# Two transformer blocks on one core: the gated branch's values and norm issued ahead of the convolution branch

## The chip, the cores and the metric

The kernel runs on one core of a Trainium2 chip. The metric is the device time of one execution in microseconds. Every time below is of this kernel on this chip. Engines are named as in the profile: PE does the matrix products (PEld its weight loads), DVE the tensor-tensor arithmetic, ACT the activations and copies, POOL little here, and SP issues the DMAs that bring weights in.

## What is computed

The program runs a first block on 512 tokens of width 1024, and then two layers of a second block, all in float32. The change lies in the first block's mixer, which is in the reference, cut to what matters:

```python
h = rms_norm(x, norm_mix_g[l]) * (1.0 + sc1) + sh1
p = h @ w_in[l]
y_a, v_first = rwkv7_mixer(p[..., :OFF_B], ...)
y_b = spatial_gating_mixer(p[..., OFF_B:OFF_C], ...)
y_c = short_conv_mixer(p[..., OFF_C:OFF_D], ...)
y_d = s5_mixer(p[..., OFF_D:OFF_G], ...)
merged = (gates[:, :, 0] * y_a + gates[:, :, 1] * y_b
          + gates[:, :, 2] * y_c + gates[:, :, 3] * y_d)
...
def spatial_gating_mixer(p, ln_w, ln_b, w_s, b_s, w_out):
    z = jax.nn.gelu(p)
    u = z[..., :D_MIX]
    v = layer_norm(z[..., D_MIX:], ln_w, ln_b, LN_EPS)
    v = v.reshape(bsz, seq // CHUNK, CHUNK, G_B, GROUP_B)
    mixed = jnp.einsum('gts,bnsgc->bntgc', w_s * mask, v) + b_s.T[None, None, :, :, None]
    return (u * mixed.reshape(bsz, seq, D_MIX)) @ w_out
def short_conv_mixer(p, conv_w, w_out):
    bg = p[..., :D_MIX]
    cg = p[..., D_MIX:2 * D_MIX]
    xin = p[..., 2 * D_MIX:]
    zp = jnp.pad(cg * xin, ((0, 0), (CONV_K - 1, 0), (0, 0)))
    y = sum(conv_w[j] * zp[:, j:j + seq] for j in range(CONV_K))
    return (bg * y) @ w_out
```

The four branches are independent of one another; all read `h`. The gated branch (`y_b`) has values `v` that are normalised and mixed over time, and gates `u`.

## The kernel before

Each float32 product is made of three products of rounded parts (`mm3`, L183): hi by hi, lo by hi, hi by lo. A weight tile is brought in by SP (`wload`, L159), ACT rounds it (whi, L160) and DVE takes the rest (wlo, L161); raw tiles have four buffers, whi and wlo three. `proj` is one such weight tile and 24 matmuls of 512 columns into one of three PSUM banks, which all products of the tag `mm` take in turn. `gelu2` (L251 to L261) is two ACT passes, two DVE passes, an ACT tanh and a DVE pass.

A scheduler puts the program's instructions into one fixed order for each engine; code written earlier has the better claim to an earlier place, and `issue_after` adds a bound to it. An engine then follows its own list and waits where something is missing.

`_first_block` (L1252) takes the mixer in this order:

- `_rwkv`: seven projections; during the sixth and seventh `_start_shift` (L476) makes the second version of `h`, eight tiles, each by DVE (L486, x), ACT (L488, hi) and DVE (L489, lo).
- `_s5_setup`: a long list of small DVE instructions on 128x8 tiles, held behind the last lo (L489).
- `_conv_branch` (L944): six projections, with a product of two (L950), two shifted taps (L957) and a gate (L959).
- `_sg_branch` (L965): first the small tables, then the values. Two weight tiles `w_in_v` (called kc 0 and 1) give 96 matmuls of 256 columns into four tiles `svp` (L979 to L984); four gelus, two norms (L996 to L1004), and the mark `sg_normed` (L1006). Then two tiles: a projection with gelu (`sgu`), the mixing (`sgm`, L1015), the bias (`sgx`, L1018), the gate (L1020) and a split.
- `_merge(K, 2, ...)`: eight output tiles, each a projection `gp` and six matmuls `yp`. Beside it, from the 27th piece on and held behind `sg_normed`, `_s5_tables` makes the tables Q and W by two `_cmul` (L1029 to L1034), twelve DVE instructions of 128x1024 elements, and then products `s5q` (L1118) and `s5k` (L1124).
- `_rwkv_shift`, `_s5_branch`, `_wkv` with the other merges, then the feed-forward part and the second block.

Of the kernel before, what the change touches and what calls it, by code (L numbers as in the profile page):

```python
# [100 lines left out]
class _Core:  # L101
# [15 lines left out]
    @contextmanager  # L117
    def tags(self, space=None, side=None, **n):

        before = dict(self.tag)  # L120
        kw = {} if space is None else {"space": space}
        if side is not None:
            kw["side"] = side
        self.npool += 1
        with self.tc.tile_pool(name=f"p{self.npool}", bufs=1, reuse_waits="tile", **kw) as p:
            self.tag.update({t: (p, c) for t, c in n.items()})
            try:
                yield
            finally:
                self.tag = before  # L130
# [209 lines left out]
def _ada(K, cols, tag=None, after=None):  # L340

    for j in cols:
        if tag is None:
            raw = K.wpool.tile([128, K.WMAX], F32, name="raw", tag="raw", bufs=4)[:, 0:1024]
        else:
            raw = K.g("ada_w", tag, shape=(128, 1024))
        _dot(K, raw, K.dram["ada_w"][j], K.c_row, K.modv[:, j:j + 1], 0.5, after)
        if j % 4 == 3:
            m = K.modv[:, j - 3:j + 1]
            K.nc.vector.tensor_tensor(m, m, K.vec("ada_b", j - 3, 4), OP.add)  # L350
        yield
# [592 lines left out]
def _conv_branch(K):  # L944
    nc, d = K.nc, K.dram
    z = []
    for i in range(2):
        cg = K.g("cg", "xr")
        nc.scalar.copy(cg, K.proj(d["w_in"][11 + 2 + i], K.h))
        nc.vector.tensor_tensor(cg, K.proj(d["w_in"][11 + 4 + i], K.h), cg, OP.mult)  # L950
        z.append(cg)
    out = []
    for i in range(2):
        y = K.g("cy", "xr")
        nc.scalar.activation(y, z[i], AF.Identity, scale=K.vec("conv_w", 4 + i))
        for j, sh in ((1, 1), (0, 2)):
            nc.vector.scalar_tensor_tensor(y[:, sh:], z[i][:, 0:S - sh], K.vec("conv_w", 2 * j + i), y[:, sh:],  # L957
                                           OP.mult, OP.add)
        nc.vector.tensor_tensor(y, K.proj(d["w_in"][11 + i], K.h), y, OP.mult)  # L959
        K.tap(f"yc{i}", y)  # L960
        out.append(K.split(y, "y"))
    return out


def _sg_branch(K, after):  # L965
    nc, d = K.nc, K.dram
    with K.tc.tile_pool(name="sgp", bufs=1, side="right") as sp:
        lnw = sp.tile([128, 2, 256], F32, name="sg_ln")
        bs = sp.tile([128, 2, 128], F32, name="sg_bs")
        ws = K._ld("sg_wsT", [128, 512], nc.sync, sp)  # L970
        for x in range(2):
            nc.sync.dma_start(lnw[:, x], d["sg_ln"][x].partition_broadcast(128))
        for g in range(4):
            nc.sync.dma_start(bs[(g % 2) * 64:(g % 2 + 1) * 64, g // 2], d["sg_bs"][g].partition_broadcast(64))
        w3 = ws.rearrange("p (g t) -> p g t", g=4)
        with K.tc.issue_after(after):
            nc.vector.tensor_tensor(w3, w3, K.tri.unsqueeze(1).to_broadcast([128, 4, 128]), OP.mult)
        vp = [K.mm("svp") for _ in range(4)]
        for kc in range(2):  # L979
            wh, wl = K.wload(d["w_in_v"][kc], 4, 256)  # L980
            for b in range(4):
                K.mm3(vp[b][:, 0:256],
                      [tuple(x[:, b * 128:(b + 1) * 128] for x in K.h[4 * kc + k]) for k in range(4)],
                      [(wh[:, k], wl[:, k]) for k in range(4)], first=kc == 0, last=kc == 1)  # L984
        vn = []
        for q in range(2):
            z = K.g("sgz", "xr")
            z3 = z.rearrange("p (b c) -> p b c", b=2)
            for b in range(2):
                K.gelu2(z3[:, b], vp[2 * q + b][:, 0:256], "xr", 256)  # L990
            st = K.col("bn_s", [128, 2, 6])
            ag = K.col("bn_a", [128, 2, 2])
            t, y = K.col("bn_t", [128, 2]), K.col("bn_y", [128, 2])
            ve = K.col("bn_v", [128, 2])
            for b in range(2):
                nc.vector.bn_stats(st[:, b], z3[:, b])  # L996
                nc.vector.bn_aggr(ag[:, b], st[:, b])
            nc.vector.tensor_scalar(ve, ag[:, :, 1], 0.25, 1e-5, OP.mult, OP.add)
            K.rsqrt(y, ve, t)
            nc.vector.tensor_scalar(y, y, 0.5, None, OP.mult)  # L1000
            for b in range(2):
                nc.vector.tensor_scalar(z3[:, b], z3[:, b], ag[:, b, 0:1], y[:, b:b + 1], OP.subtract, OP.mult)
                nc.vector.tensor_tensor(z3[:, b], z3[:, b], lnw[:, 0], OP.mult)
                nc.vector.tensor_tensor(z3[:, b], z3[:, b], lnw[:, 1], OP.add)  # L1004
                vn.append(z3[:, b])
        K.sg_normed = nc.cur_bb.bb.instructions[-1]  # L1006
        out = []
        for i in range(2):
            u = K.g("sgu", "xr")
            K.gelu2(u, K.proj(d["w_in"][7 + i], K.h), "xr")  # L1010
            ps = K.mm("sgm")
            for b in range(4):
                for h in range(2):
                    g = 2 * i + h
                    nc.tensor.matmul(ps[h * 64:(h + 1) * 64, b * 128:(b + 1) * 128],  # L1015
                                     lhsT=vn[b][:, g * 64:(g + 1) * 64], rhs=w3[:, g], start=True, stop=True)
            mx = K.g("sgx", "xr")
            nc.vector.tensor_tensor(mx.rearrange("p (b t) -> p b t", b=4), ps.rearrange("p (b t) -> p b t", b=4),  # L1018
                                    bs[:, i:i + 1].to_broadcast([128, 4, 128]), OP.add)
            nc.vector.tensor_tensor(mx, mx, u, OP.mult)  # L1020
            K.tap(f"yb{i}", mx)
            out.append(K.split(mx, "y", 0.5))
    return out


def _cmul(V, ore, oim, are, aim, bre, bim, t, conj=False):
# [225 lines left out]
def _first_block(K):  # L1252
    nc, d = K.nc, K.dram
    with ExitStack() as mix:
        tags = lambda **n: mix.enter_context(K.tags(**n))
        tags(h=16, y=8, yd=4, rk=8, cr=1)
        tags(space=PSUM, mm=3, sm=5)
        tags(side="right", tm=2)
        ada = _ada(K, range(16, 48))
        with K.tags(e=9, e4=8):  # L1260
            with K.tc.tile_pool(name="s5", bufs=1) as sp:
                tiles, rs = _rwkv(K, *_start(K))
                last = K.last
                with K.tc.issue_after(last), K.tc.issue_after(K.loaded):
                    z = _s5_setup(K, sp)
                yc = _conv_branch(K)
                yb = _sg_branch(K, last)
                acc = [K.g(f"acc{m}", "xr") for m in range(8)]
                for n, _ in enumerate(_merge(K, 2, yc, acc)):
                    if n == 26:  # L1270
                        with K.tc.issue_after(K.sg_normed):
                            tab = _s5_tables(K, sp, z)
                la, pairs = _rwkv_shift(K, tiles, rs)
            yd = _s5_branch(K, tab)
        with K.tags(rw=16, rw4=4), K.tc.tile_pool(name="rwc", bufs=1) as cp:
            la = _wkv_consts(K, cp, la)
            ya, mg = [], []
            fill = chain(_merge(K, 1, yb, acc), _merge(K, 3, yd, acc))
            for _ in range(PIECES_FIRST):
                next(fill, None)  # L1280
            for i in range(2):
                for n, _ in enumerate(_wkv(K, i, la, pairs[i][1], pairs[i][0], pairs[i][2], ya)):
                    for _ in range(int((n + 1) * PIECES) - int(n * PIECES)):
                        next(fill, None)
                    if n >= ADA_FROM and n % 2 == 0:
                        next(ada, None)
        for _ in fill:
            pass
        for _ in ada:
            pass  # L1290
        tags(mg=16)
        for _ in _merge(K, 0, ya, acc, mg):
            pass
        for m in range(8):
            K.tap(f"acc{m}", acc[m])
        K.xr = _load(K, "x", 8, "xr")
        for m in range(8):
            ps = K.proj(d["w_o"][m], mg)
            nc.vector.scalar_tensor_tensor(K.xr[m], ps, K.modv[:, 16 + m:17 + m], K.xr[m], OP.mult, OP.add)
            K.tap(f"xa{m}", K.xr[m])  # L1300
# [477 lines left out]
```

## Time and profile before

| | |
|---|---|
| median of 3 runs | 2137.5 us (2136.26 to 2139.16) |
| profiled execution | 2141.65 us |
| its span | 2139.9 us |
| mean granted clock of TensorE | 0.992 |
| PE busy | 2091.8 us, 98% |
| DVE busy | 1413.6 us, 66% |
| ACT busy | 934.5 us, 44% |
| DMA | 30.0% of 16 engines' span on the weight queue |

The span is what the profiler saw between the first and last instruction; 1.75 us of the profiled execution lie around it. Matmuls are pipelined, so each shows longer than its step: neighbours start 0.23 us apart where each is 0.39 us long. A group's "idle before" is time of that engine with nothing to do, and the arrow names what ended it. [...]

### The profile page before, as it was taken

Reading aid. Unit: us, or ns where it says so; the run is one execution under the profiler, and the core shown is the slowest. Engines: PE = TensorE matmul, PEld = TensorE weight load, DVE = VectorE, ACT = ScalarE, POOL = GpSimd, SP = SyncE. Lnnn points to the kernel's source line nnn. Section 1 sums busy time; section 2 is a strip of 40 time slices with the busy share of each in tenths; the row PEclk is TensorE's granted clock in tenths of the full one; section 3 lists DMA queues with packets and bytes.
Section 4 is the critical chain, followed back from the end, with each engine's and each line's share of the span. In section 5 each row is a group of like instructions: output and inputs, shape, how many; then the busy total and the mean of one; then the engine's idle time right before and its main releaser. Section 6 shows DMA issues by size and latency. Waiting matters only on the chain.

```text
span 2139.9 us, 29586 instructions
## 1 busy us (share of the span) xinstructions
PE 2091.8 (98%) x11542; PEld 1697.3 (79%) x11542; DVE 1413.6 (66%) x2651; ACT 934.5 (44%) x1551; POOL 21.9 (1%) x41
## 2 busy tenths in 40 slices
PE   7999999999999999999999999999999999999998
PEld 6878777778888888897778888888887678888887
DVE  7885886945644344567876756747668867575775
ACT  4433533324423232446774433424469954243433
POOL 0001000000000000000000000000000000000000
PEclk9989999999999999999999999999999999999999
DMA  8324353524322222242212322222421122323222
GB/s 319 113 72 142 107 164 104 178 88 137 111 99 93 95 99 91 97 122 87 80 60 89 99 97 91 99 93 80 136 79 41 60 79 86 102 84 105 97 81 67
DMA packets 68779, 220.47 MB, mean 103 GB/s; under 512 B 8500, under 2 KB 11604, under 8 KB 68640
## 3 DMA queue, kind: packets, MB, share of 16 engines
q1 hardware_dynamic: 65424, 210.72, 30.0%
q0 software_dynamic: 1920, 5.77, 0.9%
q8 instruction: 91, 1.49, 0.3%
q10 hardware_dynamic: 1296, 2.10, 0.3%
q14 instruction: 48, 0.39, 0.1%
HBM read 215.26 MB, written 3.30 MB: 102 GB/s over the span
## 4 chain that ended last, share of the span: by engine, by line
PE 86%; DVE 6%; ACT 4%; DMA 2%; issue 1%; SPq 0%; DVEq 0%; ACTq 0%
PE mm L183 63%; PE gp L183 7%; PE vt L183 3%; PE yp L183 2%; PE pT L1427 1%; PE po L1440 1%; DMA w_t<-w_in_t 1%; PE s L1407 1%; PE fin L183 1%; DVE wlo L161 1%; PE s L1408 1%; ACT p L1415 1%; ACT whi L160 1%; PE svp L183 1%; DVE raw L337 1%
## 5 line engine op out<-in xcount | busy, mean ns | idle before, releaser
L183 PE MATMUL mm<-hi,whi 128*128 128x512 f32 x2064 | 815.7, 396 | 2.6 <-ACT whi L160 1.6
L183 PE MATMUL mm<-hi,wlo 128*128 128x512 f32 x2064 | 816.3, 396 | 0.9 <-DVE wlo L161 0.9
L183 PE MATMUL mm<-lo,whi 128*128 128x512 f32 x2064 | 812.9, 394 | 0.9 <-DVE lo L1317 0.8
L160 ACT ACTIVATE whi<-raw 128x1024 fp32r<-128x1024 f32 (+3 forms) x338 | 347.2, 1030 | 732.0 <-PE mm L183 584.4
L161 DVE TENSOR_TENSOR wlo<-raw,whi 128x1024 fp32r<-128x1024 f32 (+3 forms) x338 | 399.8, 1185 | 173.7 <-ACT whi L160 156.8
L183 PEld LDWEIGHTS mm<-hi,whi 128*128 128x128 f32 x2064 | 389.4, 189 | 88.4 <-ACT whi L160 3.7
L183 PEld LDWEIGHTS mm<-lo,whi 128*128 128x128 f32 x2064 | 388.5, 188 | 87.8 <-DVE lo L1317 1.7
L183 PEld LDWEIGHTS mm<-hi,wlo 128*128 128x128 f32 x2064 | 388.3, 188 | 86.8 <-DVE wlo L161 1.9
L1626 DVE TENSOR_TENSOR u<-mm,spr 128x512 f32<-128x512 f32 x88 | 60.6, 688 | 80.3 <-PE mm L183 80.3
L183 PE MATMUL gp<-hi,whi 128*128 128x512 f32 x256 | 103.9, 406 | 4.8 <-ACT th L923 3.8
L183 PE MATMUL gp<-hi,wlo 128*128 128x512 f32 x256 | 103.0, 403 | 0.3 <-DVE wlo L161 0.3
L183 PE MATMUL gp<-lo,whi 128*128 128x512 f32 x256 | 102.8, 402 | 0.0
L1646 DVE TENSOR_TENSOR x<-x,mm 128x512 f32<-128x512 f32 x48 | 33.0, 687 | 95.1 <-PE mm L183 95.1
L1330 DVE SCALAR_TENSOR_TENSOR x<-mm,modv,x 128x512 f32<-128x512 f32 x32 | 24.0, 751 | 89.8 <-PE mm L183 89.8
L1627 ACT ACTIVATE cv<-u,vecs 128x512 f32<-128x512 f32 x88 | 71.3, 810 | 3.2 <-DVE u L1626 3.2
L1629 DVE SCALAR_TENSOR_TENSOR cv<-u,vecs,cv 128x510 f32<-128x510 f32 x88 | 66.0, 750 | 3.1
L1628 DVE SCALAR_TENSOR_TENSOR cv<-u,vecs,cv 128x511 f32<-128x511 f32 x88 | 65.6, 746 | 2.3 <-ACT cv L1627 2.1
L1637 ACT ACTIVATE cth<-cv 128x512 f32<-128x512 f32 x44 | 27.8, 632 | 86.5 <-DVE cv L1629 86.5
L183 PEld LDWEIGHTS gp<-hi,whi 128*128 128x128 f32 x256 | 48.7, 190 | 17.5 <-ACT th L923 5.2
L1415 ACT ACTIVATE p<-p,at_m 128x128 f32<-128x128 f32 (+1 forms) x96 | 53.4, 557 | 14.8 <-DVE at_m L1414 13.8
L183 PEld LDWEIGHTS gp<-hi,wlo 128*128 128x128 f32 x256 | 48.5, 189 | 12.2 <-DVE wlo L161 1.0
L183 PEld LDWEIGHTS gp<-lo,whi 128*128 128x128 f32 x256 | 48.8, 191 | 10.3 <-issue 0.2
(549 smaller groups left out, 2676.6 us busy)
## 6 DMA issues: line engine op xcount, KB each, us to landing
raw<-w_up SPq DMA_DIRECT2D x88, 512.0 KB, 3.3
raw<-ffn_w SPq DMA_DIRECT2D x64, 512.0 KB, 3.3
raw<-w_in SPq DMA_DIRECT2D x49, 512.0 KB, 3.5
raw<-ada_w SPq DMA_DIRECT2D x32, 512.0 KB, 4.2
raw<-w_down SPq DMA_DIRECT2D x32, 384.0 KB, 3.1
raw<-w_out SPq DMA_DIRECT2D x16, 512.0 KB, 3.4
raw<-w_down SPq DMA_DIRECT2D x16, 512.0 KB, 3.2
ada_w<-ada_w SPq DMA_DIRECT2D x14, 512.0 KB, 9.2
```

The source lines that it names most:

```text
L160: nc.scalar.activation(hi[:, :n], raw[:, :n], AF.Copy)
L161: nc.vector.tensor_tensor(lo[:, :n], raw[:, :n], hi[:, :n].bitcast(F32), OP.subtract)
L183: self.nc.tensor.matmul(out, lhsT=a, rhs=b, start=first and n == 0, stop=last and n == total - 1)
L337: K.nc.vector.tensor_tensor_reduce(raw, raw, row, scale, 0.0, OP.mult, OP.add, out)
L1330: V.scalar_tensor_tensor(K.xr[m], ps, K.modv[:, 40 + m:41 + m], K.xr[m], OP.mult, OP.add)
L1415: A.activation(p[:, 0:n], p[:, 0:n], AF.Exp, bias=nm, scale=-1.0, accum_out=l)
L1626: V.tensor_tensor(u, ps, rs, OP.mult)
L1627: A.activation(c, u, AF.Identity, bias=K.vec("conv_b_2", l * 44 + j), scale=tap(2))
L1628: V.scalar_tensor_tensor(c[:, 1:], u[:, 0:S - 1], tap(1), c[:, 1:], OP.mult, OP.add)
L1629: V.scalar_tensor_tensor(c[:, 2:], u[:, 0:S - 2], tap(0), c[:, 2:], OP.mult, OP.add)
L1637: A.activation(th, gt, AF.Tanh, scale=0.5)
L1646: V.tensor_tensor(K.xr[m], K.xr[m], ps, OP.add)
```

## The change

`_sg_branch` becomes a generator in two parts. The first part (tables, mask, values, gelus, norms, `sg_normed`) is issued ahead of `_conv_branch`, the second (the two tiles with projection, mixing, bias, gate, split) behind it. No instruction is added, removed or resized.

```diff
@@ -1004,6 +1004,7 @@
                 nc.vector.tensor_tensor(z3[:, b], z3[:, b], lnw[:, 1], OP.add)
                 vn.append(z3[:, b])
         K.sg_normed = nc.cur_bb.bb.instructions[-1]
+        yield
         out = []
         for i in range(2):
             u = K.g("sgu", "xr")
@@ -1020,7 +1021,7 @@
             nc.vector.tensor_tensor(mx, mx, u, OP.mult)
             K.tap(f"yb{i}", mx)
             out.append(K.split(mx, "y", 0.5))
-    return out
+    yield out
 
 
 def _cmul(V, ore, oim, are, aim, bre, bim, t, conj=False):
@@ -1263,8 +1264,11 @@
                 last = K.last
                 with K.tc.issue_after(last), K.tc.issue_after(K.loaded):
                     z = _s5_setup(K, sp)
+                sg = _sg_branch(K, last)
+                next(sg)
                 yc = _conv_branch(K)
-                yb = _sg_branch(K, last)
+                yb = next(sg)
+                next(sg, None)
                 acc = [K.g(f"acc{m}", "xr") for m in range(8)]
                 for n, _ in enumerate(_merge(K, 2, yc, acc)):
                     if n == 26:
```

After the change lines from L1007 on are numbered one higher.

**The order on DVE, where the eight tiles of `h` are made.** The names x_128 to x_274 are those tiles; wlo is the rest of a weight tile. Before, from the first lo on:

```order
L489 SCALAR_TENSOR_TENSOR lo<-x_128,modv,hi 128x512
L486 SCALAR_TENSOR_TENSOR x_162<-x_162,g_104,spr 128x512
L161 TENSOR_TENSOR wlo<-raw,whi 128x1024
L489 SCALAR_TENSOR_TENSOR lo<-x_135,modv,hi 128x512
L486 SCALAR_TENSOR_TENSOR x_169<-x_169,g_104,spr 128x512
L489 SCALAR_TENSOR_TENSOR lo<-x_162,modv,hi 128x512
L486 SCALAR_TENSOR_TENSOR x_208<-x_208,g_104,spr 128x512
L489 SCALAR_TENSOR_TENSOR lo<-x_169,modv,hi 128x512
L486 SCALAR_TENSOR_TENSOR x_215<-x_215,g_104,spr 128x512
L161 TENSOR_TENSOR wlo<-raw,whi 128x1024
```

With the change, from the fourth instruction of this stretch on (lo of x_128, x_162 and lo of x_135 stand ahead):

```order
L486 SCALAR_TENSOR_TENSOR x_169<-x_169,g_104,spr 128x512
L489 SCALAR_TENSOR_TENSOR lo<-x_162,modv,hi 128x512
L486 SCALAR_TENSOR_TENSOR x_208<-x_208,g_104,spr 128x512
L489 SCALAR_TENSOR_TENSOR lo<-x_169,modv,hi 128x512
L486 SCALAR_TENSOR_TENSOR x_215<-x_215,g_104,spr 128x512
L489 SCALAR_TENSOR_TENSOR lo<-x_208,modv,hi 128x512
L486 SCALAR_TENSOR_TENSOR x_268<-x_268,g_104,spr 128x512
L489 SCALAR_TENSOR_TENSOR lo<-x_215,modv,hi 128x512
L486 SCALAR_TENSOR_TENSOR x_274<-x_274,g_104,spr 128x512
L489 SCALAR_TENSOR_TENSOR lo<-x_268,modv,hi 128x512
L161 TENSOR_TENSOR wlo<-raw,whi 128x1024
L489 SCALAR_TENSOR_TENSOR lo<-x_274,modv,hi 128x512
```

The first wlo that stands here belongs before to the first projection of the convolution, and now to the first value tile, kc 0. It has moved from third place to fourteenth: behind seven lo and six x.

**The order on DVE, ahead of the first mixed tile.** s_Q and s_W are the tables' products, sgx the mixed tile that gets its bias. Before, from the second norm's first step on:

```order
L1002 TENSOR_SCALAR sgz<-sgz,bn_a,bn_y 128x256 x2
L1003 TENSOR_TENSOR sgz<-sgz,sg_ln 128x256 x2
L1004 TENSOR_TENSOR sgz<-sgz,sg_ln 128x256 x2
L1029 TENSOR_TENSOR s_Q_1370<-s_pw,s_bb 128x1024
L1018 TENSOR_TENSOR sgx<-sgm,sg_bs 128x512
L161 TENSOR_TENSOR wlo<-raw,whi 128x1024
L1020 TENSOR_TENSOR sgx<-sgx,sgu 128x512
L258 TENSOR_SCALAR gl_s<-gl_s 128x512
```

With the change, up to the same sgx:

```order
L172 TENSOR_TENSOR lo<-cy,hi 128x512
L161 TENSOR_TENSOR wlo<-raw,whi 128x1024
L1031 TENSOR_TENSOR s_tq<-s_pw,s_bc 128x1024
L1033 TENSOR_TENSOR s_W_1373<-s_pw,s_bc 128x1024
L1032 TENSOR_TENSOR s_W_1372<-s_W_1372,s_tq 128x1024
L161 TENSOR_TENSOR wlo<-raw,whi 128x1024
L258 TENSOR_SCALAR gl_s<-gl_s 128x512
L1034 TENSOR_TENSOR s_tq<-s_pw,s_bc 128x1024
L259 TENSOR_TENSOR gl_s<-gl_s,gl_x 128x512
L1035 TENSOR_TENSOR s_W_1373<-s_W_1373,s_tq 128x1024
L261 SCALAR_TENSOR_TENSOR sgu<-gl_s,gl_x 128x512
L1019 TENSOR_TENSOR sgx<-sgm,sg_bs 128x512
```

Ahead of the bias of the first mixed tile stood one of the twelve table products before; now all twelve stand there, seven of them above these rows. On PE the first products behind the last of the seven projections are now those of the values (24 matmuls of each of four tiles), then the six projections of the convolution, the two of the gates each with its mixing, and then `gp`.

## Rows read from the trace of the kernel before

**Rows 1.** Page, part 1: engine, busy time, share of the span, instructions.
```profile
PE 2091.8 (98%) x11542; PEld 1697.3 (79%) x11542; DVE 1413.6 (66%) x2651; ACT 934.5 (44%) x1551; POOL 21.9 (1%) x41
```

**Rows 2.** Page, part 4: the chain that ended last, by engine.
```profile
PE 86%; DVE 6%; ACT 4%; DMA 2%; issue 1%; SPq 0%; DVEq 0%; ACTq 0%
```

**Rows 3.** Chain in order of time, 0 to 330 us: start, us, work.
```profile
95.19 11.56 PE svp L183 x96
...
125.09 0.70 DVE sgx L1018
```

**Rows 4.** PE's waits, 51 to 260 us: total us, times, longest.
```profile
PE gp L183 <- ACT th L923: 3.8, 1, 3.8
PE sgm L1015 <- ACT gl_s L257: 2.3, 1, 2.3
```

**Rows 5.** Window: us; PE, PEld, DVE, ACT, POOL busy; PEclk, DMA, GB/s.
```profile
61.78:95.00 33.22, 33.22 (x145) 26.64 (x144) 31.82 (x129) 12.79 (x17) 0.00 (x0) 1.00 0.37 122
```

**Rows 6.** PE's timeline around the mixing: start, us, ..., idle before it.
```profile
114.62 0.69 PE L1015 MATMUL sgm<-sg_wsT,sgz 128*64 128x128 f32 x4 [2.34 <-ACT gl_s L257]
...
124.17 1.58 PE L1015 MATMUL sgm<-sg_wsT,sgz 128*64 128x128 f32 x24
125.84 0.50 PE L183 MATMUL gp<-hi,whi 128*128 128x512 f32 x1
```

**Rows 7.** Windows around drops of PEclk, columns as above.
```profile
113.78:114.28 0.50, 0.00 (x0) 0.00 (x0) 0.50 (x3) 0.33 (x1) 0.00 (x0) 1.00 0.00 0
114.28:121.06 6.78, 6.44 (x20) 4.45 (x21) 6.54 (x23) 0.63 (x1) 0.00 (x0) 0.50 0.26 79
151.67:158.66 6.99, 6.99 (x22) 5.80 (x22) 5.49 (x20) 1.43 (x2) 0.92 (x2) 0.51 0.55 169
```

**Rows 8.** PE's timeline: two other idle stretches.
```profile
466.37 0.50 PE L183 MATMUL yp<-hi,whi 128*128 128x512 f32 x1 [1.39 <-DVE th L937]
...
233.64 0.72 PE L183 MATMUL gp<-hi,whi 128*128 128x512 f32 x1 [3.79 <-ACT th L923]
```

**Rows 9.** DVE's timeline from 57.5 us on.
```profile
57.54 0.75 DVE L489 SCALAR_TENSOR_TENSOR lo<-x,modv,hi 128x512 fp32r<-128x512 f32 x1 [2.93 <-ACT hi L488]
58.20 0.75 DVE L486 SCALAR_TENSOR_TENSOR x<-x,g,spr 128x512 f32<-128x512 f32 x1
58.87 1.22 DVE L161 TENSOR_TENSOR wlo<-raw,whi 128x1024 fp32r<-128x1024 f32 x1
60.00 0.75 DVE L489 SCALAR_TENSOR_TENSOR lo<-x,modv,hi 128x512 fp32r<-128x512 f32 x1
```

**Rows 10.** ACT's timeline: a piece of hi, and the first gelu.
```profile
66.56 0.72 ACT L488 ACTIVATE hi<-x,modv 128x512 fp32r<-128x512 f32 x1 [1.67 <-DVE x L486]
...
100.90 0.37 ACT L256 COPY gl_x<-svp 128x256 f32<-128x256 f32 x1 [4.28 <-PE svp L183]
```

**Rows 11.** Window from the first lo to sgx, columns as above.
```profile
57.54:125.09 67.55, 65.21 (x331) 53.51 (x331) 57.64 (x200) 27.48 (x43) 0.00 (x0) 0.95 0.32 102
```

**Rows 12.** DVE's waits, 57.5 to 125.1 us.
```profile
DVE gl_s L258 <- ACT gl_s L257: 3.6, 1, 3.6
DVE sgx L1018 <- PE sgm L1015: 2.8, 1, 2.8
DVE wlo L161 <- ACT whi L160: 0.8, 2, 0.6
DVE cy L959 <- PE mm L183: 0.5, 1, 0.5
DVE sgz L261 <- ACT gl_s L260: 0.5, 1, 0.5
```

**Rows 13.** DVE's timeline: small ones, a table product, sgx.
```profile
78.15 1.18 DVE L217 SCALAR_TENSOR_TENSOR s_mag<-s_mag,s_x 128x8 f32<-128x8 f32 x6
...
121.09 1.22 DVE L1029 TENSOR_TENSOR s_Q<-s_pw,s_bb 128x1024 f32<-128x1024 f32 x1
125.09 0.69 DVE L1018 TENSOR_TENSOR sgx<-sgm,sg_bs 128x512 f32<-128x512 f32 x1 [2.78 <-PE sgm L1015]
```

## The prediction

> **What bounds the kernel now.** I read the shares first. PE is busy for 98% of the span, DVE for two thirds of it [rows 1], and the chain that ended last lies on PE for 86% of its length [rows 2]. So the time is the sum of PE's work, of its stretches without work, and of its stretches at half clock. A reordering without a new instruction can only act on the last two. I then looked for them where the change lies. From 51 to 260 us PE waits long only twice [rows 4]: 2.3 us for the first mixing (its normed values are late), and 3.8 us in a later stage. The first is what the change can remove. [...]
>
> **PE's sum from the last of the seven projections to the first gate product, gp.** The values are 96 matmuls in 11.56 us [rows 3], 0.12 each. The convolution's six projections take 33.22 us, 5.54 each [rows 5]; the two gate projections, of the same form, 11.08. The mixing is 32 records in all; 24 of them take 1.58 us, so 2.1 [rows 6]. Together 57.96 us. The stretch begins at 61.78 and gp begins at 125.84 [rows 5, 6], 64.06 us later; with no wait gp could begin at 119.7. So 6.1 us are there to be won (2.3 idle, 3.2 by the clock, and the rest the wait of gp for the first mixed tile).
>
> **First new term: the values wait for their weights.** With the change PE's first products behind the seventh projection need wlo of kc 0, and on DVE that stands fourteenth from the first lo, where the convolution's first wlo stood third. The instructions ahead of it are of the two kinds that start 0.66 us apart [rows 9]: 57.54 + 13 x 0.66 = 66.1, and with its own 1.22 us it is done at 67.35. ACT does not hold this back: before a piece of hi it waits for DVE's x [rows 10]. PE has three matmuls that need only hi, some 0.36 us, and then stands from 62.15 to 67.35, **5.2 us**. In before there is no stall here, because the convolution's products of three tiles could be taken as pieces of h appeared and their wlo was early.
>
> **Its clock.** A stand of 2.34 us was followed by the lower level, the fall seen 2.0 us into the idle time [rows 6, 7]; one of 1.39 us came and went at a full-speed step behind it [rows 8]. I expect 5.2 us to lose the clock. If the fall comes 2 us into the stand (64.2) and lasts 6.8 us, PE works 3.6 us of it and loses 1.8; if it falls only as work resumes, it loses 3.3. I take **2.6** between, as no row tells which. PE is then 7.8 us late and could begin gp at 119.7 + 7.8 = 127.5 (126.7 to 128.3).
>
> [...]
>
> **Second new term: DVE comes late to the first mixed tile.** gp takes the PSUM bank that the first mixing used (three banks in turn), so it waits for the bias on DVE, sgx. This was so before too: sgx starts at 125.09, gp at 125.84, 0.75 later [rows 3, 6]. With the change all twelve table products stand ahead of sgx, not one. What DVE must do first: from 57.54 to 125.09 are 67.55 us [rows 11], of which it waited 3.6 + 2.8 + 0.8 + 0.5 + 0.5 = 8.2 [rows 12]; the work with its small gaps is 59.35, that is up to 116.9. The first products' lo, x, wlo, gelus, norms and setup are the same ones in both orders. Eleven table products more, each 1.22 us long and 1.14 to the next as for the wlo of the same size [rows 9, 13], add 12.5. But a chain of small instructions costs 0.2 us a step because each needs the last [rows 13], and in the new order norms and gelus stand between them; laying the rows of the new order end to end with these durations I get 10.9, so sgx at 127.8. Then DVE waits for the first gelu: 48 of the 96 value matmuls are 5.8 us, plus the 2.6 of the clock from 67.35, is 75.7, and ACT's two passes bring 76.4 (in before 0.7 from the first of them, at 100.90 [rows 10], to DVE's step). DVE is there at about 75.8 by the same laying out: **0.6**. sgx starts at 128.4 and gp at **129.15**, 3.3 later than before. PE, ready at 127.5, stands 1.65 us there.
>
> The ends: if DVE is early, PE decides, 126.7 against 125.84, +0.9. If the small chains save nothing and all of DVE's other old waits (5.4) come back, sgx is at 116.9 + 12.5 + 5.4 = 134.8, +9.7. I take +3.3, as the old gelu wait of 3.6 stood where DVE had nothing else to do, and now it has a backlog.
>
> **What costs nothing.** The wlo of the convolution's third projection stands behind the setup's chain on DVE, at 92 to 93.5 by the same laying out, when PE wants it at about 92.6. A wait of up to 1 us there makes PE late at gp by as much, and gp is set by sgx. SP's weight loads move with the branches; the value weights are asked for earlier and the queue feeds four raw buffers as before. The tables finish some 15 us earlier, but PE had no wait for them [rows 4]. The lower clock at 151.67 comes behind the products s5q and s5k without a wait before it, so it stays [rows 7]. The 3.8-us wait for th [rows 4] hangs on weights and DVE steps long after; I let it move along with PE.
>
> **Sum.** The old wait and its clock go (-6.1), the first new stand comes (+7.8), the wait for sgx comes (+1.65): **+3.3**. The profiled execution took 2141.65 us, so it would be 2145.0; the median of the runs, 2137.5, lies 4.2 under that execution, and I put the sum on the median: **2140.8**. A measurement of this kernel can tell about 0.2%, 4.3 us, from no change; this is just inside.
>
> **Rivals.**
>
> A, slower: the stand ahead of gp loses the clock as well. At 1.65 us the stand lies between 1.39, which kept the clock, and 2.34, which lost it [rows 6, 8]; A decides if the stand comes out nearer to the second, that is if sgx is half a microsecond later than I say. Place: the gp projections from 129 on; price 3.2 to 3.4 (half of a stretch of 6.8 us), so +6.7, **2144.2**. For it: the estimate of DVE errs by 1 us easily. Against: any delay on PE earlier shortens this stand. Chance 0.33.
>
> B, DVE much later: its old waits return, up to +9.7 and the clock, 2147 to 2150. Against it speaks the backlog. Chance 0.08.
>
> C, faster: DVE is free of the table products behind gp, so the chain of weights and sums that leads to th runs earlier, and the wait of 3.79 us [rows 8] goes with its half clock, -3.8 - 3.3, with +3.3: **2133.7**. For it: 12.5 us of DVE work have moved forward by then. Against: that wait lies 100 us on, and weight loads paced by PE lie between. Chance 0.06.
>
> D, the wait goes and nothing takes its place: DVE reaches wlo of kc 0 and sgx in time because my order of waits is wrong, and gp starts near 120: -6, **2131.5**. Against: wlo's fourteenth place is plain, and DVE's work alone ends at 116.9 before any table product. Chance 0.04.
>
> **Chances.** My own case (+0.9 to +4.5, 2138.4 to 2142.0) has 0.49. Faster by over 0.2% is D, some of C, and what I don't see: 0.09. Slower by over 0.2%, above 2141.8, is A, B, and a little of my own case's upper end: 0.43. Within: 0.48. The range reaches down to 2134.5, which takes in part of C, and up to 2146.0, which takes in A with its own error; B and D stay out.
>
> **What would show it.** Right: in the changed profile PE waits about 5 us behind the seventh projection for wlo (L161), half clock follows, no wait of sgm for gl_s is left, DVE has no idle time ahead of sgx (now L1019), and gp starts near 129 behind it. Wrong: no stand at 62 us; or gp starting before 126; or a second stretch of half clock from about 130 on (A); or the wait for th much shorter than 3.8 us (C).

## The result and the profile after

The changed kernel took 2147.88 us (median of 4 runs, 2147.11 to 2148.84), the kernel before 2136.88 (4 runs beside them, 2135.36 to 2139.16): a ratio of 1.0054, 95% interval 1.0042 to 1.0066, or **+11.0 us**. The forecast was +3.3 and a time of 2140.8; its range ended at 2146.0.

The profiled execution of the changed kernel took 2147.57 us, with a mean granted clock of 0.994, as a share of full speed; half clock is a granted 0.50, as in [rows 7]. Part 1 of its page and the shares of its last chain, against [rows 1, 2]:

```profile
PE 2096.0 (98%) x11542; PEld 1695.8 (79%) x11542; DVE 1411.4 (66%) x2651; ACT 935.6 (44%) x1551; POOL 21.9 (1%) x41
PE 86%; DVE 5%; ACT 4%; DMA 2%; issue 1%; SPq 0%; DVEq 0%; ACTq 0%
```

The 11,542 matmuls are the same ones, yet they keep PE busy for 4.2 us more. This is so although the profile of before holds more half clock than that of after: from 150 to 157 us, where before fell to 0.51 [rows 7], the changed kernel was at full speed, 1.00 (second row of the windows below).

**The stretch that the change touches.** PE's waits from 51 to 270 us (engine, what waited, line, what ended it: us in total, times, longest), against [rows 4]:

```profile
PE svp L183 <- DVE wlo L161: 3.9, 1, 3.9
PE s5y L1226 <- DVE s_xb L1217: 3.3, 1, 3.3
PE svp L183 <- ACT rp L854: 0.6, 1, 0.6
```

The wait of the mixing for the gelu (2.3) is gone, the wait of the values for wlo has come, and in the place of the 3.8 us for th stands one of 3.3 for s_xb. PE's timeline in the places of [rows 6]:

```profile
62.02 0.50 PE L183 MATMUL svp<-whi,hi 128*128 128x256 f32 x2 [0.32 <-ACT whi L160]
63.10 0.38 PE L183 MATMUL svp<-whi,hi 128*128 128x256 f32 x1 [0.58 <-ACT rp L854]
67.36 0.58 PE L183 MATMUL svp<-wlo,hi 128*128 128x256 f32 x1 [3.87 <-DVE wlo L161]
126.32 1.09 PE L1016 MATMUL sgm<-sg_wsT,sgz 128*64 128x128 f32 x16
127.34 0.50 PE L183 MATMUL gp<-hi,whi 128*128 128x512 f32 x1
```

and DVE's, against [rows 9, 13]:

```profile
65.42 0.75 DVE L489 SCALAR_TENSOR_TENSOR lo<-x,modv,hi 128x512 fp32r<-128x512 f32 x1
66.08 1.22 DVE L161 TENSOR_TENSOR wlo<-raw,whi 128x1024 fp32r<-128x1024 f32 x1
126.53 0.68 DVE L1019 TENSOR_TENSOR sgx<-sgm,sg_bs 128x512 f32<-128x512 f32 x1
```

Three windows (us; busy time and count of PE, PEld, DVE, ACT, POOL; granted clock, DMA share, GB/s), against [rows 7, 11]:

```profile
67.08:70.50 3.42, 3.14 (x14) 3.15 (x15) 3.42 (x17) 0.00 (x0) 0.00 (x0) 0.54 0.45 153
150.00:157.00 7.00, 7.00 (x49) 6.36 (x49) 2.10 (x4) 1.25 (x3) 0.69 (x1) 1.00 0.26 94
57.46:126.53 69.07, 64.01 (x327) 53.19 (x327) 67.89 (x212) 26.75 (x42) 0.00 (x0) 0.98 0.29 92
```

wlo starts at 66.08, and the values go on at 67.36; PE's stand is 0.32 + 0.58 + 3.87 = 4.8 us in three pieces. 3.4 us near half clock follow. gp begins at 127.34, 1.5 later than in before (125.84 [rows 6]), and does so without a stand.

**Where the rest is.** The products `z` come much later in the program, in code that the change leaves alone. The trace lists them by tile: count, duration in ns (least, median, most), start of the first and of the last. In before (the first line is the whole span):

```profile
core 0 of [0], span 2139.9 us
L611 PE MATMUL z<-la_s,lora_s x4: 384/438/500, 267.7 to 369.0; 32*128 32x512 f32 x4
```

and in after:

```profile
core 0 of [0], span 2145.8 us
L611 PE MATMUL z<-la_s,lora_s x4: 382/442/492, 266.3 to 366.6; 32*128 32x512 f32 x4
```

At z the changed kernel's execution is 1.4 us *ahead* (before's had the second stretch of half clock). From z to the end before takes 2139.9 - 267.7 = 1872.2 us, after 2145.8 - 266.3 = **1879.5**. So 7.3 us are lost in instructions that the diff doesn't touch and that stand in the same order on PE. They are lost evenly, as a window of plain projections shows, in which PE never stops. Before:

```profile
1200.00:1500.00 300.00, 300.00 (x1301) 243.82 (x1300) 193.41 (x242) 107.38 (x131) 0.00 (x0) 1.00 0.29 93
```

After:

```profile
1200.00:1500.00 300.00, 300.00 (x1292) 242.31 (x1291) 192.11 (x240) 107.11 (x130) 0.00 (x0) 1.00 0.28 92
```

At full clock in both, 300 us hold 1301 matmuls before and 1292 after: 230.6 and 232.2 ns from one to the next.

### The profile page after: what moved, and what is told of

It is laid out like the page before. It is cut to its first block, busy times and chain, and to the rows that moved or that the text cites. A ratio compares the mean times of both kernels' runs of the same rounds, so it can differ in the third digit from the quotient of the medians.

```text
span 2145.8 us, 29593 instructions
## 1 busy us (share of the span) xinstructions
PE 2096.0 (98%) x11542; PEld 1695.8 (79%) x11542; DVE 1411.4 (66%) x2651; ACT 935.6 (44%) x1551; POOL 21.9 (1%) x41
## 4 chain that ended last, share of the span: by engine, by line
PE 86%; DVE 5%; ACT 4%; DMA 2%; issue 1%; SPq 0%; DVEq 0%; ACTq 0%
PE mm L183 63%; PE gp L183 7%; PE vt L183 3%; PE yp L183 2%; PE pT L1431 1%; PE po L1444 1%; PE s L1411 1%; PE fin L183 1%; DMA w_t<-w_in_t 1%; DVE wlo L161 1%; DMA x<-x 1%; PE s L1412 1%; ACT whi L160 1%; ACT p L1419 1%; PE svp L183 1%
## 5 line engine op out<-in xcount | busy, mean ns | idle before, releaser
L1431 PE MATMUL pT<-k_ident,p 128*128 128x128 f32 x304 | 53.9, 279 | 3.1 <-ACT p L1428 2.4
```

Of the source, the lines that this page charges most:

```text
L1431: T.transpose(pp[:, b * 128:(b + 1) * 128], p[:, b * 128:(b + 1) * 128], K.ident)
```

## The experiments

**What could differ.** Same instructions, same order on PE, same clock: what is left is where the operands lie. Ten buffers of 4160 bytes stand in a row in SBUF. I number them: raw 0 to 3, whi 4 to 6, wlo 7 to 9 of the kernel before. In the built program buffer n begins at 23840 + 4160n, so the remainders of the starts on division by 256 are 32, 96, 160, 224, 32, 96, 160, 224, 32, 96. A pool gives its buffers out as they come free in the fixed order. The change moves SP's, ACT's and DVE's instructions, and from the 24th weight tile on whi's buffers 1 and 2 are exchanged, to the program's end: where before goes round as 0, 1, 2 (regularly so from about the 65th tile on), the changed kernel goes round as 0, 2, 1. wlo's turn is the same in both, 0, 2, 1 in that part. So the **pairs** of whi and wlo that serve one projection change: before 5-9, 6-8, 4-7; after 6-9, 5-8, 4-7.

Each projection is 24 matmuls with one pair. From the start times in the traces I took the step of each (start of the next projection less its own, by 24) between 480 and 2100 us, and the median for each pair, over 55 to 59 projections (in the last two rows two levels where a pair has two; the mean there is over all projections):

| kernel | pairs whi-wlo, step in ns | mean |
|---|---|---|
| before, e1 | 5-9 229.2; 6-8 232.2; 4-7 230.1 | 230.5 |
| after, e2 | 6-9 231.9; 5-8 233.8; 4-7 230.4 | 232.0 |
| e3, e7, e8 | 2-6 227.1; 1-5 229.2; 0-4 232.9 | 229.7 |
| e5 | 2-6 227.4; 1-5 229.2; 0-4 232.6 | 229.7 |
| e6 | 2-6 227.5; 1-5 229.4; 3-7 233.4 | 230.1 |
| e4 | 9-8, 5-4, 1-0: 231.1 each in two thirds of the projections, 233.7 to 234.6 in the rest | 232.0 |
| e9 to e12 | all weight starts at one remainder: 226.7 each (seven projections of 169: 233.3) | 227.0 |

Theory 1 is that this step costs the time; its rival, that the moved stage's waits and what follows from them do.

For these runs the ten buffers got fixed names, and each weight tile takes its buffer from a written-out turn, which can be the one of before or of after (strings cut here):

```diff
+SLOT = {'raw': '0123', 'whi': '456', 'wlo': '789'}
+TURN = {"raw": ..., "whi": ..., "wlo": ...}
+    def slot(self, kind, dt):
+        i = self.used.get(kind, 0)
+        self.used[kind] = i + 1
+        return self.wpool.tile([128, self.WMAX], dt, name=kind, tag="s" + SLOT[kind][int(TURN[kind][i])], bufs=1)
-            hi = self.wpool.tile([128, self.WMAX], F32R, name="whi", tag="whi", bufs=3)
-            lo = self.wpool.tile([128, self.WMAX], F32R, name="wlo", tag="wlo", bufs=3)
+            hi, lo = self.slot("whi", F32R), self.slot("wlo", F32R)
```

**e1: the changed kernel with the old pairs** (whi's turn with 1 and 2 exchanged from the 65th weight tile on).

> The changed kernel, with one thing put back as it was before: from the 65th weight tile on (the feed-forward part and all of the second block), the three whi buffers are taken in the turn that the kernel before has there (0, 1, 2) instead of the turn of the changed kernel (0, 2, 1). PE's order is the same, instruction for instruction. Theory 1, the place of the weights: in the two traces a matmul of the 512-column projections steps every 229.2, 232.2 or 230.1 ns before, by which whi and wlo buffer it reads, and every 231.9, 233.8 or 230.4 ns after; the mean is 1.56 ns higher over some 6,200 such matmuls, 9.7 us. Then this kernel falls by 8 to 10 us from the changed one, to 2137 to 2140, and its trace shows the three old steps from the feed-forward part on. Theory 2, the moved stage itself or a slow execution: nothing falls, 2147 to 2149.

Measured: 2144.67 us (5 runs), before 2136.85 (15 runs), 1.0037 [1.0024, 1.005]. The steps came back to before's, but the time fell by only 3.2 us against the changed kernel's. Its z rows:

```profile
core 0 of [0], span 2142.9 us
L640 PE MATMUL z<-la_s,lora_s x4: 383/438/496, 268.5 to 368.9; 32*128 32x512 f32 x4
```

Behind z it takes 1874.4 us, 5.1 less than after; ahead of z this execution lost 2.2. There the clock differs: near half for some 7 us behind the stand, where after's execution had 3.4, and low once more at 154.

```profile
65.70:72.60 6.90, 5.55 (x26) 5.56 (x27) 6.72 (x26) 0.78 (x2) 0.00 (x0) 0.53 0.42 146
153.90:157.40 3.50, 3.50 (x14) 2.84 (x14) 0.00 (x0) 0.37 (x1) 0.68 (x1) 0.63 0.36 139
```

So most of the 7.3 went back with the pairs. Another 1.8 us e1 lost once, between 510 and 540 us, where the exchange begins. Half of that shows as a wait of PE for whi, the only one of PE from 505 to 545 us, where before and after have none:

```profile
PE mm L213 <- ACT whi L190: 0.9, 1, 0.9
```

Without this loss the fall would be some 5 us. Why it is no more stays open; the clock ahead of z is a likely part.

**e2: the kernel before, with the changed kernel's turn of whi.** Nothing else is moved.

> The kernel before, without the change, but with the whi buffers in the turn that the changed kernel gives them (0, 2, 1 against wlo's 0, 2, 1). Theory 1: the steps become 231.9, 233.8 and 230.4 ns and the time rises by about 10 us, to 2146 to 2148. Theory 2: no change, 2136 to 2139.

Measured: 2144.68 us (5 runs), **+7.8** on before, 1.0038 [1.0023, 1.0054], that is 4.9 to 11.5 us. Steps and time go with the turn. From z on:

```profile
core 0 of [0], span 2141.3 us
L640 PE MATMUL z<-la_s,lora_s x4: 382/442/497, 262.1 to 363.1; 32*128 32x512 f32 x4
```

2141.3 - 262.1 = 1879.2, the changed kernel's 1879.5 without the change. This shows theory 1 for the larger part. It fits the size, too: the tag mm has 3 x 2064 matmuls in all, which at 1.5 ns more are 9.3 us, an upper end, as those ahead of the new turn don't count.

**e3 and e5: both orders with the same pairs** (e3 the changed kernel, e5 the kernel before).

```diff
-SLOT = {'raw': '0123', 'whi': '456', 'wlo': '789'}
+SLOT = {'raw': '3789', 'whi': '012', 'wlo': '456'}
```

This is e3; e5 has the same places with wlo as '465' for its own turn, which makes the same pairs 2-6, 1-5, 0-4.

> The changed kernel, same order on every engine, with the ten weight buffers (each 4160 bytes, at 23840 + 4160 n) given out differently: whi has n = 0, 1, 2, wlo n = 4, 5, 6, raw the others, so that each pair of whi and wlo that is used together starts at the same remainder of 256 bytes. Theory 1a, the remainder decides: in the kernel before the one pair with equal remainders (44640 and 61280) had the shortest step, 229.2 ns; if that is the reason all three pairs step at 229.2 and the time falls by 2.8 ns x 6,200 = 17 us from the changed kernel, to about 2130. Theory 1b, the address matters in another way: three other steps between 229 and 234 ns and a time between 2129 and 2160. Theory 2: 2147 to 2149.

> The kernel before, order unchanged on every engine, with the weight buffers at the places of e3: the three pairs of whi and wlo are then the same three as in e3, so the two kernels differ by the change alone and not by the step of a matmul. Theory 1 (the step follows the places, the rest of the loss is the moved stage): the three steps are 227.1, 229.2 and 232.9 ns as in e3, mean 229.7 against 230.5 before, 0.8 ns x 6,200 to 7,000 matmuls = 5 us less than before, about 2132; e3 at 2136.5 is then 4 to 5 us slower by the stand for the first value weights. Theory 3 (all of the loss was the step): equal to e3, 2136 to 2137.

Measured: e3 2136.54 us (10 runs), 0.9999 [0.999, 1.0008] of before; e5 2133.23 (12 runs), 0.9982 [0.9973, 0.9992]. Their z rows, e3:

```profile
core 0 of [0], span 2132.9 us
L640 PE MATMUL z<-la_s,lora_s x4: 383/440/497, 264.6 to 365.0; 32*128 32x512 f32 x4
```

and e5:

```profile
core 0 of [0], span 2131.6 us
L640 PE MATMUL z<-la_s,lora_s x4: 382/440/497, 262.8 to 363.9; 32*128 32x512 f32 x4
```

From z on they take 1868.3 and 1868.8 us, the same. The whole effect of the order lies ahead of z, and the medians differ by 2136.54 - 2133.23 = **+3.3**. That is the forecast's sum, though the two ratios lie only 0.0017 apart, with some 0.0013 of uncertainty by their intervals (1 to 6 us), and the two profiled executions differ by 1.3 us. Turn and order add up: 7.8 + 3.3 = 11.1, for 11.0 measured; with each known to some 3 us, so close a fit is luck. A narrower form of theory 1 falls here: these pairs are all four places apart, at equal remainders, and have three steps.

**e4: pairs one place apart** (the changed kernel, raw '2367', whi '159', wlo '048').

> As the run before it, with whi at n = 1, 5, 9 and wlo at n = 0, 4, 8: every pair has the remainders (96 and 32) of the pair with the longest step so far (44640 and 57120, 233.8 ns). Theory 1a: all three pairs step at about 233.8 ns, 1.8 above the mean of the changed kernel, +11 us, 2159. Theory 1b: steps that don't repeat that number. Theory 2: 2147 to 2149.

Measured: 2147.76 us (4 runs), 1.0053 [1.0036, 1.0071]. That is the time of after, and so is the mean step, 232.0. But each pair has two steps in this kernel, 231.1 in some stretches and 233.7 to 234.6 in others, and changes between them only where other products stand between. Two windows of plain projections, both at full clock with PE never idle, hold 386 and 391 matmuls:

```profile
1290.00:1380.00 90.00, 90.00 (x386) 72.48 (x385) 61.53 (x78) 34.21 (x42) 0.00 (x0) 1.00 0.30 94
1400.00:1490.00 90.00, 90.00 (x391) 73.19 (x390) 51.97 (x64) 28.97 (x35) 0.00 (x0) 1.00 0.28 92
```

The pairs, the remainders (96 with 32) and, in the built program, the places of most of the tiles of h are the same in both stretches. So the places of whi and wlo alone don't set the step here, and neither do their remainders.

**e6: the kernel before, one pair exchanged** (raw '0489', whi '123', wlo '576': 3-7 for 0-4).

> The kernel before with whi at n = 1, 2, 3 and wlo at n = 5, 6, 7: the pairs 1-5 and 2-6, which stepped 229.2 and 227.1 ns in e3, and 3-7, not seen yet, in place of 0-4 (232.9 ns). Theory 1a: two steps repeat at 229.2 and 227.1. If the third lies at 227 to 229 the mean falls to 228.0 to 228.5, 14 to 17 us less than the kernel before, 2120 to 2123; at 233 it is as e5.

Measured: 2135.26 us (10 runs), 0.9986 [0.9976, 0.9996]. 2-6 and 1-5 kept their steps within 0.4 ns, and 3-7, also four places apart, takes 233.4. Except in e4, a pair carries its step from program to program.

The span behind z goes with the mean step in all these runs: 1868 to 1869 us at 229.7 ns (e3 and e5, and e7 and e8 below), 1870.7 at 230.1 (e6), 1872.2 at 230.5 (before), and 1879.2 to 1879.5 at 232.0 (after, e2, e4). That is some 4.8 us for each ns. Only e1 lies off this, 2.2 us above before, of which 1.8 were lost where its exchange begins.

**e7 and e8: the forecast's two waits taken away**, both on e3's places. e7 loads the first value tile ahead of the second version of h, so that its wlo no longer stands behind seven lo on DVE. e8 then holds the tables back until the first mixed tile is split, so that sgx has no table products ahead of it.

```diff
+            K.first_v = K.wload(d["w_in_v"][0], 4, 256)
...
-            wh, wl = K.wload(d["w_in_v"][kc], 4, 256)
+            wh, wl = K.first_v if kc == 0 else K.wload(d["w_in_v"][kc], 4, 256)
```

```diff
+            if i == 0:
+                K.sg_first = nc.cur_bb.bb.instructions[-1]
...
-                        with K.tc.issue_after(K.sg_normed):
+                        with K.tc.issue_after(K.sg_first):
```

> e3 (the change, with its places) with one thing moved: the weight tile kc 0 of the values is loaded and split ahead of the second version of h, so that wlo of kc 0 stands on DVE ahead of its eight lo and not behind seven. The stand of 4.8 us behind the seventh projection should go, and with it 1.7 to 3.4 us of half clock. Theory 1 with DVE as the next bound (my second term): the twelve table products still stand ahead of sgx, DVE has no idle time from 57 us on, sgx stays near 126, PE stands 4 to 6 us ahead of gp and loses the clock there; 1 us less than e3 at most, 2135.5 to 2137. Theory 1 without that bound: 6 us less, 2130.

> e7 with the twelve table products held behind the split of the first mixed tile, about where they stood before. If both of my terms were real and one hid the other, now both are gone: gp begins near 121 us instead of 127.4, 6 us less than e3, 2130 to 2131, and 1 to 2 us less than e5. If DVE was no bound: equal to e7.

Measured: e7 2130.67 us (10 runs), 0.9964 [0.9954, 0.9975], 5.9 below e3 by the medians. PE's waits from 51 to 140 us in e3:

```profile
PE svp L213 <- DVE wlo L191: 3.9, 1, 3.9
PE svp L213 <- ACT rp L883: 0.6, 1, 0.6
PE gp L213 <- DVE sgx L1048: 0.4, 1, 0.4
```

in e7:

```profile
PE svp L213 <- ACT hi L517: 0.8, 1, 0.8
PE svp L213 <- ACT gl_s L287: 0.3, 1, 0.3
```

The stand is gone, gp begins at 123.30, and sgx at 122.21, 4.3 earlier than in after. That is not because DVE no longer waits for PE: in after it waits for nothing from its first lo to sgx. Part of it is the order, which came out different from what was expected: in e7 only ten of the twelve table products stand ahead of sgx, 2.3 us less work. e8: 2131.58 us (7 runs), 0.9968 [0.9956, 0.9981], the same as e7, though its sgx starts at 117.98; from the first lo to gp its profile has 63.3 us, e7's 63.5. **The ten tables ahead of sgx in e7 cost nothing.** What all twelve would cost without the stand was not run.

**e9 and e11: the kernel before with every start at one remainder.** Only the last value weights of the second block are 1040 elements wide (4 x 260), and this width sets all ten buffers. With their eight row blocks in quarters of two, 1024 elements do (4096 bytes, a multiple of 256). e9 has a pad ahead that puts weights and h at 160, e11 none, which puts both at 32.

```diff
-    WMAX = 1040
+    WMAX = 1024
+        self.wpool.tile([128, 32], F32, name="pad", tag="pad", bufs=1)
...
-                wl = [K.wload(src[ch, kc], 4, w) for kc in range(2)]
+                parts = 4 if w > 256 else 2
+                per = 8 // parts
+                wl = [K.wload(src[ch, kc], per, w, "wide" if kc == 3 else None) for kc in range(parts)]
```

> The kernel before with every weight buffer 4096 bytes long instead of 4160, so that all ten start at the same remainder of 256 bytes, 160, which is also that of most tiles of h and is the remainder of the pair 2-6 (227.1 to 227.5 ns in e3, e5 and e6). The three weight tiles of 1040 columns in the second block come as six quarters in place of three halves twice over, for which one stand of a few us is allowed. Theory 1a (the remainders of whi, wlo and the moving tile decide the step): all three pairs step at 227.1 ns, 3.3 less than before, 6,200 to 7,000 matmuls: 20 to 23 us less, 2115 to 2120 with that stand. Theory 1b (the full address matters): three different steps, mean 228 to 233 ns, 2122 to 2157.

> e9 with everything behind the weights 128 bytes lower: all ten buffers and most tiles of h at remainder 32. If only the remainders relative to one another count, the same steps and time as e9. If 32 as such is slow (the pair 0-4, both at 32, stepped 232.9 ns, with h at 160), steps near 232.9 and about 2157.

Measured: e9 2129.98 us (5 runs), 0.9962 [0.9948, 0.9975]; e11 2127.28 (4 runs), 0.9953 [0.9938, 0.9968]. The window of plain projections in e9:

```profile
1200.00:1500.00 300.00, 299.53 (x1319) 246.77 (x1318) 196.81 (x248) 110.57 (x137) 0.00 (x0) 1.00 0.28 93
```

1319 matmuls where before had 1301, and e11 has as many: 226.7 ns in all pairs. With the starts equal, 160 and 32 give the same step. The tiles of h matter too: in both, seven of the 169 projections step 233.3 ns with the same weight buffers, and those are the ones whose tiles of h start at another remainder than the weights (96 against 160 in e9). Both times lie some 10 us above the 2115 to 2120 expected of e9. The quarters give back about 10 us, between 800 and 1000 us (below).

**e10 and e12: the changed order, the first values early, one remainder.** e10 joins e7's load and e9's buffers. e12 takes thirds (three, three and two row blocks) for the quarters.

```diff
-                parts = 4 if w > 256 else 2
-                per = 8 // parts
-                wl = [K.wload(src[ch, kc], per, w, "wide" if kc == 3 else None) for kc in range(parts)]
+                if w > 256:
+                    per = 3
+                    wl = [K.wload(src[ch, kc][:, 0:n * w], n, w, t) for kc, (n, t) in
+                          enumerate(((3, None), (3, None), (2, "wide")))]
```

> e7 (the change, with wlo of kc 0 ahead of the second version of h) with the buffers of e9. Theory 1a: 6 us less than e9, as e7 is less than e3, 2109 to 2114. Theory 1b: 6 us less than e9, wherever that lies; against e9 it repeats what the early first weight is worth.

> e10 with the three wide weight tiles of the second block in thirds (780, 780 and 520 columns), so that two of three buffers serve them, as before, and the last third has its own small one. In e10's trace the quarters cost two stands near 930 and 978 us, each followed by half clock, about 8 to 10 us against e7 by the shift from 800 to 1000 us. All steps of 512 columns stay at 226.7 ns. If the third buffer is what the quarters lacked, both stands fall to those of the kernel before and the time falls by 6 to 9 us, to 2113 to 2116; if not, 2122.

Measured: e10 2122.26 us (4 runs), 0.9925 [0.9909, 0.9942], 8 us above what was expected; e12 **2119.25** (5 runs), 0.992 [0.9904, 0.9935] of the 2136.28 beside it: 17.0 us faster than before, and faster than both kernels. PE's waits from 920 to 990 us in e10, where the value weights come:

```profile
PE fgc L1498 <- issue: 3.4, 1, 3.4
PE vt L185 <- DVE wlo L163: 3.3, 1, 3.3
```

and in e12:

```profile
PE fgc L1502 <- issue: 3.4, 1, 3.4
PE vt L185 <- DVE wlo L163: 0.3, 1, 0.3
```

The thirds took away one of two waits, for 3.0 us of medians where 6 to 9 were expected; the other (1.0 us in after) stayed and was not followed further. With the same 11,542 matmuls, PE is busy for 23.7 us less than in before [rows 1], of which some 3 are before's second stretch of half clock:

```profile
PE 2068.1 (98%) x11542; PEld 1693.9 (80%) x11542; DVE 1408.0 (66%) x2654; ACT 934.3 (44%) x1554; POOL 21.8 (1%) x41
```

## Why the prediction was wrong

**The step that failed** is in its first paragraph: the time is the sum of PE's work, its stretches without work and its stretches at half clock, and "a reordering without a new instruction can only act on the last two". PE's work itself grew, by 1.5 ns on average for each of some 6,200 matmuls of the projections. The paragraph on what costs nothing made the same omission: it followed the weight loads' times through the raw buffers, and not which whi and wlo each projection gets. e2 shows this part alone to be worth +7.8.

Point by point:

- **The old wait and its clock (-6.1).** Right in kind, as no wait of the mixing for gl_s is left, but too large: the profile that it was read from had a long stretch of half clock. From the first mixing to gp it has 125.84 - 114.62 = 11.2 us [rows 6], and the other five profiles with before's order (e2, e5, e6, e9, e11) have 9.9, with 3.4 us of half clock in place of 6.8 and the same wait. So some 4.7 were to be won. The 3.2 by the clock among the 6.1 are an estimate, half of the 6.44 us that PE was busy at clock 0.50 [rows 7]; in e2 half of the time at 0.50 is 1.7. Three rows of e2, the last a window as above:

```profile
113.84 0.44 PE L1044 MATMUL sgm<-sg_wsT,sgz 128*64 128x128 f32 x4 [2.33 <-ACT gl_s L287]
123.69 0.50 PE L213 MATMUL gp<-hi,whi 128*128 128x512 f32 x1
114.31:117.72 3.41, 3.41 (x10) 2.23 (x11) 3.27 (x11) 0.63 (x1) 0.00 (x0) 0.50 0.27 71
```

- **The first new stand (5.2).** Right in place and cause: wlo was forecast for 66.1 and done at 67.35, and began at 66.08, with PE going on at 67.36. It came as 4.8 us, since the three matmuls that need only hi show 0.9 us of work, where I had 0.36.
- **Its clock (2.6 of 6.8 us).** The stand lost the clock, as forecast. In after's execution 3.4 us followed near half clock, about 1.6 lost (0.46 x 3.42); in e1's it was twice as long. 2.6 lies between.
- **PE ready at 127.5.** Right: gp began at 127.34 without a wait.
- **The second new term, sgx at 128.4 and PE's stand of 1.65.** Mis-sized: sgx began at 126.53, 1.9 earlier, and was done 0.1 us ahead of gp. From the first lo at 57.46 DVE was busy for 67.89 of 69.07 us, so its backlog was there, without the gelu wait of 0.6 that I added; the rest is my laying end to end, which came out too long. PE lost nothing to it in after and 0.4 us in e3, and e8 gained nothing on e7.
- **The sum of +3.3.** It is what e3 and e5 measure at equal steps, in part by luck: the gain of 6.1 was 1.4 too large and the loss of 1.65 ahead of sgx did not come, and these two errors nearly cancel. z starts at 263.7 on average over the six profiles with before's order (261.6 to 267.7) and at 266.9 over the four with the changed order and its stand (264.6 to 268.5), 3.2 later, though the two ranges overlap; gp was only 1.5 later in the pair first compared.
- **The rivals.** None happened. A's second loss of clock ahead of gp had no stand to follow; B's old waits stayed away; C: the wait for th went, but one of 3.3 us for s_xb took its place; D: the stand came. That the result lies where B had put it (2147 to 2150) is chance: it comes from the turn of the buffers, which was no rival at all.

With its two faults mended, early value weights and equal buffers, the moved order is worth something: e7 lies 2.6 us below e5 at the same pairs, and e10 lies 7.7 below e9, whose buffers it has, and 5.0 below e11, all in medians.

## What to carry to other kernels

After a reordering, compare the step of instructions that were *not* touched, in a window where the engine never waits: 1301 against 1292 matmuls in 300 us told more than all the waits. A pool that gives out buffers as they come free can change which operands meet for the rest of the program, so look at the turn of its buffers as well as at the order of the instructions. If many matmuls stream from pool buffers, try a buffer size that puts all the operands at one remainder (here 4096 for 4160 bytes, -3.8 ns a matmul, or 1.7%, against before).

## What was not expected of the hardware

- **A 512-column matmul's step depends on where its operands lie in SBUF**: 226.7 ns with all starts at one remainder of 256, up to 234.6 otherwise, at full clock with PE busy for over 99.8% of the windows. A pair's step repeats within 0.4 ns in other programs, but in e4 the same pairs have two steps (231.1 and 233.7 to 234.6). What exactly decides it stays open (and no run tries 256 against another divisor): neither the distance of the pair (four places, with 227.1 to 233.4 in e3 and e6) nor the remainders of whi and wlo alone (e4) do, and a change of the tiles of h alone moves it from 226.7 to 233.3 (e9).
- Stretches near half clock varied between the profiled executions of nearly the same order. With before's order the stretch at 151 us in the first profile [rows 7] was missing from those of e2 and e5 (1.00 from 150 to 157 us in both), and behind the same stand it was 3.4 us long in after and about 6.8 in e1. Behind the old wait of 2.3 us it was 6.8 us long in the first profile and 3.4 in the five others. The execution that the first profile shows lies 4.8 us over before's median.
